# Twelve instead of eight pairs of projection tiles by seven half products in an encoder layer, with some sums and row exchanges by transfers and shifted priorities

## The chip, the core and the metric

The kernel runs on one core of one Trainium2 chip. The core has five engines with queues of their own: TensorE (PE, matmuls; PEld is its weight load), VectorE (DVE), ScalarE (ACT), GpSimd (POOL) and SyncE (SP, which here only issues transfers). Transfers are issued from SP's queue, and from POOL's where they add to what is at the destination (`accum_op`). On-chip memory is SBUF; matmuls write to eight banks of PSUM. The metric is the device time of one execution in microseconds (us), and the median of several executions is compared.

## What is computed

One encoder layer on x of 512 tokens by 1024 features, in float32. The reference, cut to what matters:

```python
proj = h @ w_in[l]
qa, ka, va, qb, kb, vb = jnp.split(proj, SPLITS, axis=-1)   # 1024, 256, 256, 768, 768, 768 wide
# partial rotary on qa, ka, qb, kb (first 16 of 64 dims)
o_a = windowed_gqa_sink(qa, ka, va, a_sink[l])              # 16 heads, 4 kv heads, |i-j| <= 128
o_b = dilated_mixture(qb, kb, vb)                           # 3 groups of 4 heads, merged by denominators
gates = jax.nn.sigmoid(h @ w_gate[l] + b_gate[l])
g_a, g_b = jnp.split(gates, N_BRANCH, axis=-1)
mixed = g_a * (o_a @ w_br_a[l]) + g_b * (o_b @ w_br_b[l])
h = layer_norm(DN_ALPHA * h + mixed @ w_out[l], ln1_g[l], ln1_b[l])
f = (jax.nn.silu(h @ w_ff_gate[l]) * (h @ w_ff_up[l])) @ w_ff_down[l]
h = layer_norm(DN_ALPHA * h + f, ln2_g[l], ln2_b[l])
```

## The kernel before

**Arithmetic.** Each float32 operand is split into a high part (a copy to the type fp32r) and a low part (the difference). A product is three matmuls: high by high, high by low, low by high. The copy for the high part goes to ACT or DVE, the subtraction for the low part always to DVE.

**Dense tiles.** The weights lie in DRAM as units of 128 x 1024. A projection tile (128 output features by all 512 tokens) is `feat_x` (L533): eight slices of the inner dimension times three matmuls of 512 columns (L523 to L525), so 24. Its weights come in two halves of 128 x 512 (256 KB), each loaded on SP's queue and split by `split` (low part at L399). A tile is finished either straight from PSUM (gates by `gate`, L1238; the first query tiles by `rotate`) or copied to SBUF by ACT (`in_sbuf`).

**Pairs.** `pair_x` computes two tiles at once as a two by two block product by Strassen's scheme in Winograd's form: the inner dimension and the tokens are each halved, and seven half products do the work of eight. A half product is four slices times three matmuls of 256 columns (L639 to L641). On the weights' side it needs A11, A12 and A22 as loaded, S1 and S3 (sums of two loaded parts, made by a load on SP and a second, accumulating load issued from POOL, L387), and S2 = S1 + A11 and S4 = A12 + S2 (sums by `form`, with `tt`, on DVE at L544). All seven are then split (`parts`: the high part on ACT at L373, the low part on DVE at L544). On x's side the four sums T1 to T4 are made once by `x_forms` (the step X) and split into `XP`. The order of products is A11, A12, S2, S1, S3, S4, A22. Results are gathered from two banks by four ACT copies of 256 columns (`keep`, L647) and two DVE operations (a `tt` and L662). The feed-forward half uses the same scheme in `quad` (L1690 to L1692).

**Rotary.** `rotate` turns a whole tile on DVE by four operations. For tiles in SBUF, `turn_rows` (the step R) gathers the 16 rows of each head that turn into one tile G by small transfers on SP (L712), makes the exchanged rows H from G by a shuffle on DVE (L715), multiplies both by cosines and sines, adds, and sends the rows back (L723).

**Attention.** `unit_a` (steps A0 to A3, four blocks each) does near attention for one kv head: scores, a masked reduction on DVE (L1022) that needs a sink column copied by POOL (L1020), exponentials on ACT (L1026), normalisation on ACT or DVE (L961, L963), transposes on PE (L973) and products with the values (L1039, L1040). The outputs go to DRAM (`oaD`) and come back in the steps O with an accumulating load (L1308). `unit_b` (B0 to B3) does the dilated mixture for one head slot.

**Gates.** Of 16 gate tiles, two (8 and 9) are computed along with the first tiles, and the rest in the order 10 to 15, 0 to 7. Gates 11 to 15, which come out of pairs, are put away to DRAM (L1229) and fetched back in the branch stage (L1401).

**What sets the order.** The kernel's text records operations with a priority; `Program.run` then plays them against a model of the engines and emits them, so the order on each engine is fixed when the program is built. An operation's priority is `pr.T`, the matmul time recorded so far, plus its own offset (weight loads and splits have -130, `LOOK`). `ORDER` lists the steps: VA, V0 and V12 are values, q, k, Q and K query and key tiles, g gates, P a pair, R turned rows, L a change of the room for weights. Rooms bound how far work runs ahead: `N_WSA` slots for loaded weights, `N_WHLA` for split ones, two slots for each half product. After the attention come the branches, the output projection with the first layer norm, and the feed-forward half with the second. They are the same in both versions.

Of the kernel before, what the change touches and what calls it, by code (L numbers as in the profile page):

```python
# [15 lines left out]
P = 128  # L16
# [35 lines left out]
BIAS = 0.2  # L52
SPARE, SPARE2 = 12, 12
ROOMS = {2: dict(whl=16), 3: dict(whl=20, ws=8)}
# [39 lines left out]
PACK = -60.0  # L94
BY_DMA = ()
AWAY = range(8, 16)
N_WSA, N_WHLA = 8, 16
PAIR_DMA = ()
# [210 lines left out]
def dve(n, fast=False, extra=0.0):  # L309
    return 0.069 + (0.00052 if fast else 0.00104) * n + extra  # L310
# [21 lines left out]
def hybrid_layer(ctx: ExitStack, tc: tile.TileContext, wpack, xT, xtok, sink, bgate,  # L332
# [260 lines left out]

    def pair_x(ua, ub):

# [105 lines left out]

    def turn_rows(tiles):


        c, s_ = packed()
        G, H = slot(), slot()
        n = 32 * len(tiles)
        gs = []
        for i, R in enumerate(tiles):
            for h in range(2):  # L710
                gs.append((G, 2 * i + h))
                op([(SP, 0.1)], lambda e, R=R, i=i, h=h: nc.sync.dma_start(  # L712
                    G.t[32 * i + 16 * h:32 * i + 16 * h + 16], R.t[64 * h:64 * h + 16]), reads=[(R, 1), (R, 2)], writes=[gs[-1]], prio=EV)
        g, h_ = (lambda: G.t[0:n]), (lambda: H.t[0:n])
        op([(DVE, dve(S, extra=0.03))], lambda e: nc.vector.stream_shuffle(h_(), g(), SHUF2), reads=gs, writes=[H], prio=EV)  # L715
        op([(DVE, dve(S))], lambda e: nc.vector.tensor_tensor(g(), g(), c.t[0:n], op=ALU.mult),
           reads=[*gs, *[(c, i) for i in range(4)]], writes=gs, prio=EV)
        op([(DVE, dve(S))], lambda e: nc.vector.tensor_tensor(h_(), h_(), s_.t[0:n], op=ALU.mult),
           reads=[H, *[(s_, i) for i in range(4)]], writes=[H], prio=EV)
# [155 lines left out]

    def turned_values(u, nt, turn_by=0, done=None):

        src = []
        w = S // nt
        for i in range(2):  # L880
            ps = done
            if i or not done:
                ps = bank("dense")
                feat_x(ps, unit(u + i))
            t = slot()

            def evac(e, t=t, ps=ps):
                for a in range(2):
                    s = ps.t.rearrange("p (r t i a) -> p a t r i", a=2, r=2, t=nt)[:, a]
                    d = t.t.rearrange("p (t a r i) -> p a t r i", a=2, r=2, t=nt)[:, a]  # L890
                    if turn_by:
                        copy(e, d[:, turn_by:], s[:, :nt - turn_by])
                        copy(e, d[:, :turn_by], s[:, nt - turn_by:])
                    else:
                        copy(e, d, s)

            op(cp_alts(S, True, 0.3 if turn_by else 0.1)[:2 if turn_by else 1], evac, reads=[ps], writes=[t], prio=VAL if i else NORM)
            src.append(t)
        res = []
        for b in range(NR):  # L900
            pb = bank("tb")

            def turn(e, pb=pb, b=b):
                for i in range(2):
                    nc.tensor.transpose(pb.t[:, i * P:(i + 1) * P], src[i].t[:, b * P:(b + 1) * P], ident.t)

            op([(PE, 0.18)], turn, reads=[*src, ident], writes=[pb])
            res.append(value_split(pb))
        return res
# [57 lines left out]
    def turned_probs(srcs, toks):  # L967

        pb = bank("tb")

        def go(e):
            for i, s in enumerate(srcs):
                nc.tensor.transpose(pb.t[:, i * P:(i + 1) * P], s(), ident.t)  # L973

        op([(PE, 0.36)], go, reads=[*toks, ident], writes=[pb])
        h, l = slot(F32R, "att"), slot(F32R, "att")
        op(cp_alts(S, True), lambda e: copy(e, h.t, pb.t), reads=[pb], writes=[h, (l, "room")])
        op([(DVE, dve(S))], lambda e: nc.vector.tensor_tensor(l.t, pb.t, f32(h.t), op=ALU.subtract),
           reads=[pb, h], writes=[l])
        return h, l  # L980

    def turned_pairs(srcs, toks):
# [6 lines left out]

        op([(PE, 0.36)], go, reads=[*toks, ident], writes=[pb])  # L990
        xs = []
# [59 lines left out]
    def unit_b(hs, q, k, v0, v1, v2):  # L1051
# [98 lines left out]

        dil = []
        for half in range(2):
            xs = turned_pairs([lambda r=r, g=g: pd[r // 2].t[:, (r % 2) * 256 + (g - 1) * P:(r % 2) * 256 + g * P]
# [4 lines left out]
            def pv(e, half=half, xs=xs, od=od):  # L1158
# [6 lines left out]
            op([(PE, 4 * pe(256))], pv, reads=[y for x in xs for y in vtok(x)] + [  # L1165
                y for vs in (v1, v2) for t in vs[2 * half:2 * half + 2] for y in vtok(t)], writes=[od])
            t = slot(F32, "att")
            dil.append(t)
            part = lambda od=od: od.t.rearrange("p (r i a) -> p r a i", r=2, a=2)
            sums = lambda t=t: t.t[0:64, 0:256].rearrange("p (r i) -> p r i", r=2)  # L1170
# [12 lines left out]
        for ms in ((1, 2), (3, 0)):  # L1183
# [17 lines left out]
            op([(PE, 4 * 0.1195)], pv, reads=[hh, ll] + [x for m in ms for x in vtok(v0[m])], writes=[o])  # L1201
        t = slot(F32, "att")
        op(cp_alts(S, True), lambda e: copy(e, t.t[0:64], o.t[64:128]), reads=[o], writes=[t])
        a = 64 * (hs % 2)
        op([(DVE, dve(S))], lambda e: nc.vector.tensor_tensor(t.t[0:64], o.t[0:64], t.t[0:64], op=ALU.add),
# [59 lines left out]
    for f in range(N_ALONG):  # L1265
        gate(8 + f, ps=along[f])
    ka = k_near(psk, 4)
    qa = q_near(psq, 4, (0, 0))
    load(mB, maskb, prio=0)
# [42 lines left out]
    def units_of(w):  # L1312
# [8 lines left out]
        if w[0] == "q":  # L1321
            return U_QA + i, lambda t: qa.extend(q_post(t, 4, ((i // 2) % 2,) * 2))
        if w[0] == "k":
            return U_KA + i, lambda t: ka.extend(k_post(t, 4))
        f = (env["gate"] + 8) % 16
# [3 lines left out]
    def step(w):  # L1329
        if w == "X":  # L1330
            x_forms()
        elif w == "L":
            op([(POOL, 0.0)], lambda e: pr.limits.update(ws=N_WS, whl=N_WHL), after=[env["mark"]])
        elif w[:2] == "P:":
            both = [units_of(x) for x in w[2:].split(",")]
            for (u, f), t in zip(both, pair_x(*[u for u, _ in both])):
                if u < U_GATE:
                    env["turn"].append((t, f))
                else:
                    f(t)  # L1340
        elif w[:2] == "T:":
            u, f = units_of(w[2:])
            env["turn"].append((in_sbuf(u), f))
        elif w == "R":
            tiles = [t for t, _ in env["turn"]]
            turn_rows(tiles)
            done_rows.update(tiles)
# [7 lines left out]
        elif w[0] == "q":  # L1355
            i = int(w[1])
            kv = (i // 2) % 2
            qa.extend(dense_q(U_QA + i, 4, (kv, kv)))
        elif w == "k1":
            ka.extend(dense_k(U_KA + 1, 4))  # L1360
        elif w[0] == "A":
            g = int(w[1])
            for b in range(NR):
                unit_a(g, b, qa[4 * g:4 * g + 4], ka[g], env["va"])
        elif w[0] in "gG":
# [3 lines left out]
        elif w[0] in "QK":  # L1369
            pair, g = int(w[1]), int(w[2])  # L1370
            u, f = units_of(w)
            env["turn"].append((in_sbuf(u), f))
        elif w == "V0":
            env["v0"] = turned_values(U_V0, 8, 1)
# [9 lines left out]

    for w in ORDER.split():
        step(w)

    def free_all(e):
# [166 lines left out]
    def turn_h1(t, j, c0, c1, tok):  # L1555
# [6 lines left out]

        op([(PE, 0.36)], go, reads=[z, ident], writes=[pb], prio=NORM)
        c = slice(t * P, (t + 1) * P)
# [481 lines left out]
```

## Time and profile before

| | us |
|---|---|
| median of 3 runs | 727.84 (727.19 to 729.8) |
| span of the profiled execution, first to last instruction | 725.8 |
| length of the attention part, the branch part and the feed-forward part (about) | 340, 80 and 306 |

The profiled execution's span is 2.0 us less than the median, which is what lies around the instructions. The three parts of the span are: the projections and attentions (0 to about 340 us), the branches and the first layer norm (to about 420 us), and the feed-forward half. In the page's row for an engine stand busy us, the share of the span and the number of instructions. In the rows of groups stand line, engine, operation, output<-inputs, shapes and count, then busy us and mean ns of one, then the idle time before them and what ended it. In the timeline a row is the start, the length and the instruction.

### The profile page before, as it was taken

Reading aid. Unit: us, or ns where it says so; the run is one execution under the profiler, and the core shown is the slowest. Engines: PE = TensorE matmul, PEld = TensorE weight load, DVE = VectorE, ACT = ScalarE, POOL = GpSimd, SP = SyncE. Lnnn points to the kernel's source line nnn. Section 1 sums busy time; section 2 is a strip of 40 time slices with the busy share of each in tenths; the row PEclk is TensorE's granted clock in tenths of the full one; section 3 lists DMA queues with packets and bytes.
Section 4 is the critical chain, followed back from the end, with each engine's and each line's share of the span. In section 5 each row is a group of like instructions: output and inputs, shape, how many; then the busy total and the mean of one; then the engine's idle time right before and its main releaser. Section 6 shows DMA issues by size and latency. Waiting matters only on the chain.

```text
span 725.8 us, 14412 instructions
## 1 busy us (share of the span) xinstructions
PE 717.3 (99%) x4767; PEld 666.2 (92%) x4767; DVE 655.6 (90%) x1408; ACT 471.4 (65%) x1077; POOL 134.0 (18%) x297
## 2 busy tenths in 40 slices
PE   9999999999999999999999999999999999999995
PEld 7889999989988888988888999999999999999985
DVE  6999999889997898898967898899999999899987
ACT  5757798868778665666534666756666566666821
POOL 0021211111100731450020021111112211212000
PEclk9999999999999999999999999999999999999998
DMA  8978788856577689965681499676888888979302
GB/s 256 309 155 202 191 213 246 211 135 172 170 192 185 160 228 253 309 217 185 216 209 44 116 267 228 154 199 155 200 254 212 193 215 225 258 184 200 97 30 87
DMA packets 88010, 140.30 MB, mean 193 GB/s; under 512 B 11136, under 2 KB 24064, under 8 KB 87936
## 3 DMA queue, kind: packets, MB, share of 16 engines
q1 hardware_dynamic: 74336, 114.87, 51.7%
q0 software_dynamic: 13328, 24.39, 20.5%
q8 instruction: 37, 0.61, 0.3%
q14 instruction: 37, 0.30, 0.1%
q10 hardware_dynamic: 272, 0.13, 0.1%
HBM read 114.97 MB, written 7.60 MB: 169 GB/s over the span
## 4 chain that ended last, share of the span: by engine, by line
PE 99%; DVE 1%; DVEq 0%; issue 0%
PE ps L1692 10%; PE ps L1691 9%; PE ps L1690 9%; PE ps L523 9%; PE ps L524 9%; PE ps L525 9%; PE ps L1901 4%; PE ps L1903 4%; PE ps L1902 4%; PE ps L641 3%; PE ps L640 3%; PE ps L639 3%; PE ps L973 3%; PE ps L1480 3%; PE ps L1481 3%; PE ps L1482 3%
## 5 line engine op out<-in xcount | busy, mean ns | idle before, releaser
L373 ACT ACTIVATE sl<-sl 128x512 fp32r<-128x512 f32 (+3 forms) x419 | 230.8, 583 | 59.7 <-DVE sl L544 31.1
L544 DVE TENSOR_TENSOR sl<-sl,sl 128x512 fp32r<-128x512 f32 (+3 forms) x378 | 222.4, 621 | 5.1 <-ACT sl L373 3.4
L373 ACT ACTIVATE sl<-ps 128x256 f32<-128x256 f32 (+5 forms) x209 | 88.7, 445 | 91.6 <-PE ps L1692 56.8
L387 POOL DMA_DIRECT2D sl<-wpack x60 | 53.1, 885 | 342.9 <-DMA sl<-wpack 118.2
L1691 PE MATMUL ps<-sl,sl 128*128 128x256 f32 x352 | 96.8, 275 | 0.0
L1692 PE MATMUL ps<-sl,sl 128*128 128x256 f32 x352 | 96.8, 275 | 0.0
L1690 PE MATMUL ps<-sl,sl 128*128 128x256 f32 x352 | 96.8, 275 | 0.0
L523 PE MATMUL ps<-x,sl 128*128 128x512 f32 (+1 forms) x241 | 93.9, 389 | 0.0
L525 PE MATMUL ps<-x,sl 128*128 128x512 f32 (+1 forms) x241 | 91.4, 379 | 0.0
L524 PE MATMUL ps<-x,sl 128*128 128x512 f32 (+1 forms) x209 | 79.5, 380 | 0.0
L1690 PE MATMUL ps<-x,sl 128*128 128x256 f32 x264 | 72.6, 275 | 0.0
L1691 PE MATMUL ps<-x,sl 128*128 128x256 f32 x264 | 72.6, 275 | 0.0
L1692 PE MATMUL ps<-x,sl 128*128 128x256 f32 x264 | 72.6, 275 | 0.0
L1691 PEld LDWEIGHTS ps<-sl,sl 128*128 128x128 f32 x352 | 67.6, 192 | 0.1
L1690 PEld LDWEIGHTS ps<-sl,sl 128*128 128x128 f32 x352 | 67.6, 192 | 0.1
L1692 PEld LDWEIGHTS ps<-sl,sl 128*128 128x128 f32 x352 | 67.6, 192 | 0.0
L399 DVE TENSOR_TENSOR sl<-sl,sl 128x512 fp32r<-128x512 f32 x94 | 62.8, 682 | 1.8 <-ACT sl L373 1.3
L525 PEld LDWEIGHTS ps<-x,sl 128*128 128x128 f32 x241 | 45.9, 190 | 6.5
L1690 PEld LDWEIGHTS ps<-x,sl 128*128 128x128 f32 x264 | 50.6, 192 | 0.4
L1691 PEld LDWEIGHTS ps<-x,sl 128*128 128x128 f32 x264 | 50.6, 192 | 0.4
L523 PEld LDWEIGHTS ps<-x,sl 128*128 128x128 f32 x241 | 46.0, 191 | 5.4 <-ACT sl L373 0.3
L1692 PEld LDWEIGHTS ps<-x,sl 128*128 128x128 f32 x264 | 50.7, 192 | 0.0
(172 smaller groups left out, 1851.0 us busy)
## 6 DMA issues: line engine op xcount, KB each, us to landing
sl<-wpack SPq DMA_DIRECT2D x249, 256.0 KB, 3.9
sl<-wpack POOLq DMA_DIRECT2D x60, 256.0 KB, 5.3
sl<-sl SPq DMA_DIRECT2D x110, 128.0 KB, 3.1
wf<-wpack SPq DMA_DIRECT2D x51, 256.0 KB, 5.2
wf<-wpack POOLq DMA_DIRECT2D x24, 256.0 KB, 6.2
oa<-sl SPq DMA_DIRECT2D x32, 128.0 KB, 3.6
sl<-sl SPq DMA_DIRECT2D x68, 32.0 KB, 2.6
sl<-oa SPq DMA_DIRECT2D x8, 256.0 KB, 5.1
```

The lines of the kernel that those rows point to most:

```text
L373: nc.scalar.activation(dst, src, AF.Copy)
L387: op([(POOL, 1.0)], lambda e: nc.gpsimd.dma_start(b.t, src2, accum_op=ALU.add), reads=[b], writes=[b], prio=prio, moves=1.65)
L399: op([(DVE, dve(S))], lambda e: nc.vector.tensor_tensor(l.t, src.t, f32(h.t), op=ALU.subtract), reads=[src, h], writes=[l], prio=prio, abs ...
L523: mm(o, a, x0, start=(k == 0 and begins), stop=False, skip_group_check=split)
L524: mm(o, a, x1, start=False, stop=False, skip_group_check=split)
L525: mm(o, b, x0, start=False, stop=(k == nk - 1), skip_group_check=split)
L544: op([(DVE, dve(w))], lambda e: nc.vector.tensor_tensor(dst(), x(), y(), op=o), reads=reads, writes=writes, prio=prio)
L1690: mm(o, wh, pairs(bh[k]()), start=(first and k == 0), stop=False, skip_group_check=True)
L1691: mm(o, wh, pairs(bl[k]()), start=False, stop=False, skip_group_check=True)
L1692: mm(o, wl, pairs(bh[k]()), start=False, stop=(k == 3), skip_group_check=True)
L1901: mm(ps.t, x0, pairs(w[0].t), start=(first and m == 0), stop=False, skip_group_check=True)
L1902: mm(ps.t, x0, pairs(w[1].t), start=False, stop=False, skip_group_check=True)
```

## The change

The number of steps P or D in `ORDER` goes from 8 to 12. A pair can now mix a query or key tile with a gate. Pairs marked D make the sums S2 and S4 by accumulating transfers from SBUF to SBUF, issued from POOL, instead of by DVE. Steps marked r make H by further small transfers on SP instead of the shuffle. A step may carry `@n`, which shifts the priority of all that it records by n (us of matmul time, negative is earlier). Gates 8 to 10 are now put away as well. Three constants change, and two costs that the planner assumes for transposes. `SUM_BY_DMA` stays empty and the step PV isn't used, so that what hangs on them (in `unit_b` and `turned_values`) emits nothing; `qa` and `ka` become dictionaries.

```diff
-SPARE, SPARE2 = 12, 12
+SPARE, SPARE2 = (10, 12)
 ORDER = """
-VA q1 A0 q2 q3 g X P:k1,q4 R A1 P:q5,g P:q6,q7 R A2 P:g,g A3 P:g,g L P:Q00,K00 R V12 P:Q01,K01 R P:Q02,K02 R V0 B0 Q10 K10 R Q11 K11 R B1 O O Q12 K12 R O O B2 B3 O O O O g8
+q1@-778 VA@-8 X@-496 A0@-58 q2@-14 P:q3,g@6 R@-96 D:k1,q4@8 R@72 P:q5,Q01@-338 D:q6,q7@-15 D:g,g@21 r@471 P:g,Q00 L@-4 A1@-8 P:g,K00@-17
+A3@19 A2@-16 R@321 V12@15 P:g,K01@13 R@9 P:Q02,K02@4 R@13 V0@50 B0@1 P:K10,Q12@9 R@-52 K11@5 P:Q10,Q11 R@6 B1@-20 O@-83 O@1 O@-56 O@-622
+K12@6 g@-17 O@-20 r@-507 O@34 O@30 g@16 g@34 g@22 B2 O P:g,g@-15 B3@1 g@-43 g@5
 """
-FORMS = -60.0
+FORMS = -120.0
-N_WSA, N_WHLA = 8, 16
+N_WSA, N_WHLA = (8, 18)
...
-    def pair_x(ua, ub):
+    def pair_x(ua, ub, by_dma=False):
...
         def form(key, of, x, y):
+            if by_dma:
+                a, b = W[of], W[x if y == of else y]
+                op([(POOL, 1.0)], lambda e: nc.gpsimd.dma_start(a.t, b.t, accum_op=ALU.add), reads=[a, b], writes=[a],
+                   prio=-LOOK, moves=1.65)
+                W[key] = a
+                return
             tt(lambda: W[of].t, lambda: W[x].t, lambda: W[y].t, ALU.add, [W[x], W[y]], [W[of]], S, -LOOK)
...
-    def turn_rows(tiles):
+    def turn_rows(tiles, by_dma=False):
...
+        hs_ = [H]
+        if by_dma:
+            hs_ = []
+            for i, R in enumerate(tiles):
+                for h in range(2):
+                    for z in range(2):
+                        hs_.append((H, 4 * i + 2 * h + z))
+                        op([(SP, 0.1)], lambda e, R=R, i=i, h=h, z=z: nc.sync.dma_start(
+                            H.t[32 * i + 16 * h + 8 * z:32 * i + 16 * h + 8 * z + 8], R.t[64 * h + 8 - 8 * z:64 * h + 16 - 8 * z]),
+                           reads=[(R, 1), (R, 2)], writes=[hs_[-1]], prio=EV)
+        else:
+            op([(DVE, dve(S, extra=0.03))], lambda e: nc.vector.stream_shuffle(h_(), g(), SHUF2), reads=gs, writes=[H], prio=EV)
...
-        op([(PE, 0.36)], go, reads=[*toks, ident], writes=[pb])
+        op([(PE, 0.436)], go, reads=[*toks, ident], writes=[pb])
...
     def gate(f, ps=None):
...
+        if f in AWAY:
+            put_away(f)
...
-        elif w[:2] == "P:":
+        elif w[:2] in ("P:", "D:"):
...
-            for (u, f), t in zip(both, pair_x(*[u for u, _ in both])):
+            for (u, f), t in zip(both, pair_x(*[u for u, _ in both], w[0] == "D")):
...
-        elif w == "R":
+        elif w in "Rr":
             tiles = [t for t, _ in env["turn"]]
-            turn_rows(tiles)
+            turn_rows(tiles, w == "r")
...
     for w in ORDER.split():
+        w, _, later = w.partition("@")
+        pr.T += float(later or 0)
         step(w)
+        pr.T -= float(later or 0)
```

More of the change, by code (lines that the diff above doesn't have):

```diff
@@ L95 @@
 BY_DMA = ()
+SUM_BY_DMA = ()
 AWAY = range(8, 16)
-N_WSA, N_WHLA = 8, 16
+N_WSA, N_WHLA = (8, 18)
 PAIR_DMA = ()
@@ L873, in scores, with turned_values @@
         return go, [(qt, "h"), (qt, "l"), (kt, "h"), (kt, "d"), (kl, "h"), (kl, "d")]
-    def turned_values(u, nt, turn_by=0, done=None):
+    def turned_values(u, nt, turn_by=0, done=None, made=None):
         src = []
@@ L880, in turned_values, with order @@
         for i in range(2):
+            if made:
+                t, z = slot(), made[i]
+                def order(e, t=t, z=z):
+                    s = z.t.rearrange("p (r t i) -> p t r i", r=4, t=nt)
+                    d = t.t.rearrange("p (t r i) -> p t r i", r=4, t=nt)
+                    copy(e, d[:, turn_by:], s[:, :nt - turn_by])
+                    copy(e, d[:, :turn_by], s[:, nt - turn_by:])
+                op([(ACT, act(S) + 0.1)], order, reads=[(z, 1), (z, 2)], writes=[t], prio=VAL if i else NORM)
+                src.append(t)
+                continue
             ps = done
@@ L1151, in unit_b @@
         dil = []
+        add_up = hs in SUM_BY_DMA
+        E = [slot(F32, "att"), slot(F32, "att")] if add_up else []
         for half in range(2):
```

44 lines of the change are left out of this document (30 added, 14 removed).

## The prediction, made before the run

> **What bounds the kernel now.** I read the table of cores first, then the page's busy line and its chain, then what TensorE (PE) waited for.
>
> ```profile
> core 0: 725.8 us, clock 0.996
> PE 717.3 (99%) x4767; PEld 666.2 (92%) x4767; DVE 655.6 (90%) x1408; ACT 471.4 (65%) x1077; POOL 134.0 (18%) x297
> PE 99%; DVE 1%; DVEq 0%; issue 0%
> PE ps L459 <- DVE eps L510: 1.2, 1, 1.2
> ```
>
> The chain that ended last is PE almost from end to end, at full granted clock, and the list of PE's waits has one entry, 1.2 us at the very start. So time can only come out of the number of matmuls and their spacing, and anything else matters only once it makes PE wait. A busy PE is not proof of that, since matmul ends are modelled; the proof is the spacing of their starts. From the timeline of PE, first and last of 62 rows of dense projections, and then of 127 rows of half products:
>
> ```profile
> 19.69 0.38 PE L525 MATMUL ps<-x,sl 128*128 128x512 f32 x1
> ...
> 32.85 0.38 PE L523 MATMUL ps<-x,sl 128*128 128x512 f32 x1
> 423.83 0.28 PE L1691 MATMUL ps<-sl,sl 128*128 128x256 f32 x1
> ...
> 437.90 0.28 PE L1691 MATMUL ps<-sl,sl 128*128 128x256 f32 x1
> ```
>
> A 512-wide matmul costs 13.16/61 = 0.2157 us, a 256-wide one 14.07/126 = 0.1117 us; the second stretch also shows that half products run with no hole for 14 us on end.
>
> The second engine near its limit is VectorE (DVE). By stage (columns: window, length, busy us of PE, PEld, DVE, ACT, POOL, then clock, DMA share, GB/s):
>
> ```profile
> 0.00:80.00 80.00, 78.81 (x440) 69.63 (x441) 72.09 (x157) 54.61 (x120) 12.45 (x25) 1.00 0.80 222
> 80.00:200.00 120.00, 120.00 (x899) 114.54 (x898) 110.54 (x259) 96.35 (x237) 18.80 (x52) 1.00 0.73 195
> 200.00:340.00 140.00, 140.00 (x775) 125.39 (x774) 121.79 (x336) 96.64 (x248) 43.84 (x152) 1.00 0.77 217
> 420.00:680.00 260.00, 260.00 (x2037) 251.56 (x2037) 245.66 (x472) 167.82 (x361) 49.42 (x57) 1.00 0.82 207
> ```
>
> DVE is at 90%, 92% and 87% in the three stretches that the change rearranges, and at 245.66/260 = 94.5% in the feed-forward stretch, where PE waits for nothing. 94.5% is therefore a load that this kernel is seen to carry.
>
> **The change part by part.** *Four more pairs.* Two dense projection tiles are 48 matmuls of 512 columns, 48 x 0.2157 = 10.36 us. A pair is seven products of 12 matmuls of 256 columns, 84 x 0.1117 = 9.38 us. One pair saves 0.98 us and four save 3.90 us, all on the path. The number of transposes, scores and attention products is unchanged, and the feed-forward half is not touched. The constants 0.36 to 0.436 and 0.18 to 0.218 only tell the planner what a transpose costs; they add no instruction.
>
> *What the pairs ask of DVE and ACT.* The rows, within 0 to 340 us:
>
> ```profile
> L399 DVE TENSOR_TENSOR sl<-sl,sl 128x512 fp32r<-128x512 f32 x70 | 47.0, 682 | 1.8 <-ACT sl L373 1.3 <-DMA sl<-sl 0.4
> L544 DVE TENSOR_TENSOR sl<-sl,sl 128x512 f32<-128x512 f32 x16 | 10.9, 683 | 0.0
> L544 DVE TENSOR_TENSOR sl<-sl,ps 128x512 f32<-128x512 f32 x8 | 5.5, 685 | 0.1
> L662 DVE SCALAR_TENSOR_TENSOR sl<-ps,sl 128x256 f32<-128x256 f32 x8 | 3.3, 418 | 0.7 <-ACT sl L1026 0.6
> L715 DVE STREAM_SHUFFLE sl<-sl 64x512 f32<-64x512 f32 x7 | 5.1, 732 | 0.0
> L373 ACT ACTIVATE sl<-sl 128x512 fp32r<-128x512 f32 x151 | 90.4, 622 | 16.8 <-DVE sl L747 7.2 <-DVE sl L570 2.7 <-DVE sl L1211 1.7
> L647 ACT ACTIVATE sl<-ps 128x256 f32<-128x256 f32 x32 | 12.0, 375 | 3.7 <-PE ps L641 3.6
> ```
>
> Two dense tiles need four low parts, 4 x 0.68 = 2.73 us of DVE. A pair needs seven, the two weight sums S2 and S4 (the 16 rows of L544, two for each of the eight pairs) and two merges of results: 9 x 0.68 + 0.69 + 0.42 = 7.25 us. So a pair adds 4.5 us of DVE, four add 18.1. Three pairs marked D hand both sums to transfers: 6 x 0.683 = 4.1 us less. Two exchange steps marked r lose their shuffle: 1.5 us less. Net +12.5 us of DVE. On ACT a pair adds three copies and four evictions, 3 x 0.62 + 4 x 0.375 = 3.4 us, 13.5 for four, less four evictions of dense tiles that go (0.6 each), about 11 us on an engine with 92 us to spare before 340 us.
>
> Where this falls decides whether it is hidden. Up to the first dilated unit there are nine pairs where eight were, three of them with transferred sums: 4.5 - 4.1 - 0.7, no change. After that come three new pairs in the stretch 200 to 340: 121.8 + 3 x 4.52 - 0.73 = 134.6 us of DVE in 140 - 2.9 = 137 us, or 98%. That is over 94.5%, unless work moves to ACT. What can move there are the copies and scalings that the planner may give to either engine:
>
> ```profile
> 200.00:340.00 140.00, 8.61 (x22) 1.00 0.77 217
> 200.00:340.00 140.00, 5.89 (x19) 1.00 0.77 217
> ```
>
> These are DVE's copies (L375) and normalisations (L963) in that stretch, 14.5 us together; to fall back to 94.5% only 5.1 us of it must move, and ACT has 137 - 96.6 - 8 = 32 us free there. I cost the added DVE and ACT work at nothing; without that cover it is 134.6/0.945 - 137 = 5.4 us.
>
> *Sums by transfer and POOL's queue.* Issues, with the median time to landing, and POOL's own instruction (min/median/max ns):
>
> ```profile
> sl<-wpack POOLq DMA_DIRECT2D x60, 256.0 KB, 5.3
> sl<-oa POOLq DMA_DIRECT2D x8, 256.0 KB, 7.5
> sl<-sl SPq DMA_DIRECT2D x68, 32.0 KB, 2.6
> L387 POOL DMA_DIRECT2D sl<-wpack x60: 848/862/1563, 34.8 to 653.5; - x60
> L1020 POOL COPY sl<-nsink x64: 178/184/1847, 40.1 to 217.0; 128x1 f32<-128x1 f32 x64
> ```
>
> Four pairs bring 8 accumulating loads and the D pairs 6 accumulations within SBUF: 14 x 0.86 = 12 us of POOL, which is 18% busy. An accumulation from SBUF to SBUF is not in the trace; its cost to the path lies between nothing and the delay of a chain. In a D pair S2 waits for S1, and S4 for S2. Each sum takes 0.86 + 5.3 = 6.2 us (by the slower row 8.4) where DVE took 0.68, so S4 is ready 11.0 to 15.4 us later. Behind a waiting accumulation in POOL's order stand the next pair's S1 and S3 and the sink copies of L1020, which DVE's score reductions and so PE's transposes wait for. What hides it is the lead of the weights: 18 slots for split halves (N_WHLA, 16 before) are nine products of 12 x 0.1117 = 1.34 us, 12.1 us. I take the nearer row, 11.0, which that lead just covers: cost nothing.
>
> The Trainium skill, "DMA: Bandwidth & Descriptors", section "Anatomy of one DMA", gives such a POOL-issued transfer 2.0 us plus bytes over 436 GB/s, an estimate of 2.6 us for 256 KB. By that the chain would be 2 x (0.86 + 2.6 - 0.68) = 5.6 us later and well covered. The 5.3 us row is twice that, and I go by the row.
>
> A rule speaks against the change. The Trainium skill, "SBUF — State Buffer", section "SBUF: two separate sides", says that a DVE copy in a two-port mode locks GpSimd out, so that a POOL-issued transfer's descriptors wait. The issue row agrees that an issue can stretch, from 862 to 1563 ns. If all 14 stretched so far, POOL would lose 9.8 us, and PE nothing while the lead holds.
>
> *Row exchanges, gates, order.* The r steps replace a shuffle by 16 and 4 small transfers on SP's queue; each lands in some 2.6 us, beside the ones that the step already waits for, so at best 0.73 us shorter and at worst 20 issues long for the weight loads behind them. Gates 8, 9 and 10 now go to DRAM and come back: 6 x 256 KB. All traffic added (12 weight parts, 6 sums, 6 gate moves, 256 KB each, and the rows) is 6.6 MB, where 340 us at 200 GB/s move 68; the DMA share of 0.73 to 0.80 has room for 10%. Bounds for the two together: nothing, to about 2 us if one load comes late; I take nothing. The shifted priorities reorder work that PE has plenty of; the forms of x, which must now be done for the first pair earlier, had their first sums at 7.6 us already:
>
> ```profile
> L544 DVE TENSOR_TENSOR sl<-sl x4: 415/417/424, 7.6 to 14.7; 128x256 f32<-128x256 f32 x4
> ```
>
> **Sum.** 3.90 us off a span of 725.8 us is 721.9. The median of the runs, 727.84, is 2.0 us above the span, so the floor is 723.9. I add 0.4 us for small new waits, an estimate between none and the single 1.2 us that the trace has: **724.3 us**.
>
> **The rivals.** *DVE becomes the bound between the dilated units* (for: 98% before anything moves; also DVE is nearly full before 80 us, where the pair of q3 adds 4.5. Against: 14.5 us can move, 94.5% is carried). At the full 5.4 us: 723.9 + 5.4 = 729.3; half of it gives 726.6.
>
> *The chain of transferred sums outlasts the lead* (slower). Place: the three D pairs, before the near attention is done. Each falls short by 15.4 - 12.1 = 3.3 us if such an accumulation lands like the oa row. Three times that is 9.9 us: 733.8 us. It decides from a landing of 5.9 us on (2 x (0.86 + 5.9 - 0.68) = 12.1). For: 7.5 is seen. Against: other ready work stands in PE's order between the products, and 5.3 is the median of 60.
>
> *The pairs do not save what they should*: if half products in this stage were spaced 0.1175 us apart half of the gain would go, 725.9. Against it is the 0.1117 us row, from the same kind of product.
>
> **How the numbers follow.** Saved and covered 0.60 (723.5 to 725.3), DVE bound 0.25, sums late 0.12, spacing 0.03. A measurement of this kernel can tell about 0.5% from no change, 3.6 us, so "faster" begins at 724.2: within the likeliest case. Waits under 0.3 us in all would put it there. I split that case 0.38 faster, 0.22 within; DVE and spacing lie within (0.28), of which 0.02 counts as faster for a repeat of the runs' own scatter; late sums are slower. Faster 0.40, within 0.48, slower 0.12. The range starts 0.9 us under the floor (the runs lie 0.65 under to 2.0 over their median) at 723.0 and takes in the DVE case up to 729.3; late sums stay out.
>
> **What would show it.** Right: the matmuls of L639 to L641 rise from 672 to 1008 and the dense ones fall by 192, PE's list of waits stays near one entry, DVE over 92% in 200 to 340 with fewer copies of L375 and L963. DVE bound: PE waits on DVE lines after 200 us. Late sums: PE waits before 200 us on splits that follow a sl<-sl transfer of POOL. The prediction falls if the first matmuls, the tail after the last one, or the feed-forward stretch change in length, for none of these was given a term.

## The result: slower, and the profile after

| | before | after |
|---|---|---|
| median of 5 runs, us | 727.84 (727.19 to 729.80) | 740.15 (737.72 to 743.21) |
| span of the profiled execution, us | 725.8 | 737.7 |

The ratio is 1.0167, with a 95% interval of 1.0145 to 1.0189: slower by 1.7%, outside the predicted range. From the table of cores, the page and its chain of waits, in the order in which they were shown of before:

```profile
core 0: 737.7 us, clock 0.996
PE 718.9 (97%) x4911; PEld 668.8 (91%) x4911; DVE 665.3 (90%) x1418; ACT 482.4 (65%) x1109; POOL 145.4 (20%) x311
PE 77%; DMA 4%; DVE 4%; POOL 3%; ACT 2%; issue 2%; SPq 0%; DVEq 0%; ACTq 0%; POOLq 0%
```

No engine is busier than forecast. DVE gained 9.7 us over the whole span (12.5 were forecast), ACT 11.0 (11), POOL 11.4 (12). But the chain, 99% PE before, now goes through transfers, DVE, POOL and ACT for some 15% of the span. (It can be followed back only to 59.1 us, so 8% are not covered.) The list of what PE waited for had one entry; now its first five are:

```profile
PE ps L1196 <- DVE sl L1030: 2.6, 3, 1.2
PE ps L890 <- DVE sl L791: 2.5, 2, 2.3
PE ps L1239 <- DVE sl L1010: 1.7, 1, 1.7
PE ps L462 <- DVE eps L513: 1.2, 1, 1.2
PE ps L528 <- DVE sl L402: 1.1, 1, 1.1
```

The fourth is the old one at the start. The pairs themselves did what they should. From the groups by line, the dense matmuls of before and then of after, and one group of the half products (L639 before, L648 after), in each kernel:

```profile
L523 PE MATMUL ps<-x,sl 128*128 128x512 f32 (+1 forms) x241 | 93.9, 389 | 0.0
L639 PE MATMUL ps<-sl,sl 128*128 128x256 f32 x128 | 35.5, 277 | 0.0
```

```profile
L526 PE MATMUL ps<-x,sl 128*128 128x512 f32 (+1 forms) x177 | 68.4, 386 | 0.1
L648 PE MATMUL ps<-sl,sl 128*128 128x256 f32 x192 | 53.4, 278 | 0.0
```

64 dense matmuls fewer on each of three lines, 192 in all, and half as many half products again. So the 3.9 us were saved, and about 16 us of new holes (stretches in which PE stands or runs slowly) lie over them. Adding up, over all rows of PE's timeline, what each distance between two starts exceeds the distance in an undisturbed run of its width (0.216, 0.1625 and 0.1117 us for 512, 384 and 256 columns, 0.109 for a transpose) gives 8.2 us before and 24.1 us after. The difference of 15.9, less 3.9, is 12.0; the spans differ by 11.9. By place the excess of after is 4.9 us from 40 to 80 us, 1.8 from 140 to 160, 6.3 from 260 to 300, 4.8 from 300 to 340, 0.9 from 400 to 420, and at most 0.7 in any other 20 us once the start is over. From the table by stage (columns as before):

```profile
40.00:60.00 20.00, 17.52 (x111) 15.75 (x110) 16.90 (x30) 11.19 (x20) 4.60 (x8) 1.00 0.92 227
140.00:160.00 20.00, 19.18 (x107) 16.49 (x106) 17.57 (x44) 13.07 (x34) 3.57 (x12) 1.00 0.87 221
260.00:280.00 20.00, 16.40 (x102) 14.03 (x101) 18.23 (x38) 10.67 (x27) 5.70 (x12) 1.00 0.82 200
320.00:340.00 20.00, 18.11 (x101) 15.65 (x101) 16.63 (x46) 14.22 (x34) 7.53 (x34) 1.00 0.59 195
```

PE waits on DVE in nearly all of these, but DVE has idle time in each of the windows. So the question is what DVE waited for. Its list of waits, from 38 to 60 us, 250 to 280 and 280 to 345:

```profile
DVE sl L547 <- DMA sl<-wpack: 2.8, 1, 2.8
...
DVE sl L735 <- DMA sl<-sl: 3.3, 1, 3.3
...
DVE sl L402 <- ACT sl L376: 4.3, 2, 3.8
DVE st L1158 <- POOL st L1151: 3.0, 2, 2.6
```

These holes have the same shape: one instruction of DVE stands on a late transfer, or on a late copy by POOL or ACT. DVE's order is fixed when the program is built, so what PE needs stands behind the waiting instruction. The first case can be followed row by row. The sum of a pair waited 2.8 us at 44.9 us for its accumulating load. DVE then hardly paused up to 62 us and did not win the time back, and PE stood at 56 us. From the timelines of DVE and then of PE:

```profile
47.67 0.69 DVE L547 TENSOR_TENSOR sl<-sl,sl 128x512 f32<-128x512 f32 x1 [2.82 <-DMA sl<-wpack]
57.71 1.40 DVE L791 TENSOR_TENSOR sl<-sl,sl 64x512 fp32r<-64x512 f32 x2
...
55.86 0.38 PE L528 MATMUL ps<-x,sl 128*128 128x512 f32 x1
58.55 0.35 PE L890 MATMUL ps<-sl,sl 128*128 128x256 f32 x1 [2.31 <-DVE sl L791]
```

This first hole is not a fixed part of the change. The load was issued at 39.2 us and landed at 47.6. Six of the kernels below keep this order, and their edits act only after 50 us. In their profiles the same load was issued at 37.0 to 38.0 us and landed at 43.8 to 45.0, DVE waited for it 0.1 us at most, and the excess from 40 to 80 us is at most 2.0 us instead of 4.9. So of seven profiles with this order only the one shown here has this hole, and why the load was late in it stays open.

In the case at 260 us the shuffle of a step R (L735) waits for gathers of rows (L721), which SP issued one behind the other up to 257.4 us. SP's timeline from 220 to 262 us, of after and then of before: the first and the last row of 62 issues in each, and between them a run of twelve moves of the dilated unit and, of after, the last two gathers of that step:

```profile
219.87 0.59 SPq L743 DMA_DIRECT2D sl<-sl  x1
...
243.74 9.28 SPq L831 DMA_DIRECT2D sl<-sl  x12
...
256.79 1.15 SPq L721 DMA_DIRECT2D sl<-sl  x2
...
261.60 0.68 SPq L731 DMA_DIRECT2D sl<-sl  x1
```

```profile
220.05 0.59 SPq L811 DMA_DIRECT2D sl<-sl  x1
...
242.79 8.44 SPq L811 DMA_DIRECT2D sl<-sl  x12
...
261.56 0.57 SPq L1307 DMA_DIRECT2D sl<-oa  x1
```

DVE's waits of before, from 250 to 280 us, have the same entry:

```profile
DVE sl L715 <- DMA sl<-sl: 1.6, 2, 1.3
```

The twelve issues take 9.28 us after and 8.44 before, 0.77 and 0.70 us each, and the rows of the 62, with the short pauses within them, add up to 39.9 and 39.4 of some 42 us, so the queue has next to no room there in both kernels. The change hardly adds to it at this place; from 100 to 200 us SP's issues take 75.0 us (124 of them) where they took 65.3 (114). DVE waited for late rows in before as well, 1.3 us at most, and PE never noticed. After, it is 3.3 us, and PE does. A queue with next to no room, and a lead that was just enough for one order, is what the profile of before had to tell and what the prediction did not read from it.

### The profile page after: what moved, and what is told of

It reads as the page before. It is cut to its first block, busy times and chain, and to the rows that moved or that the text cites. A ratio compares the mean times of both kernels' runs of the same rounds, so it can differ in the third digit from the quotient of the medians.

```text
span 737.7 us, 14857 instructions
## 1 busy us (share of the span) xinstructions
PE 718.9 (97%) x4911; PEld 668.8 (91%) x4911; DVE 665.3 (90%) x1418; ACT 482.4 (65%) x1109; POOL 145.4 (20%) x311
## 4 chain that ended last, share of the span: by engine, by line
PE 77%; DMA 4%; DVE 4%; POOL 3%; ACT 2%; issue 2%; SPq 0%; DVEq 0%; ACTq 0%; POOLq 0%
PE ps L1747 9%; PE ps L1746 9%; PE ps L1748 9%; PE ps L650 4%; PE ps L649 4%; PE ps L648 4%; PE ps L1957 4%; PE ps L1959 4%; PE ps L1958 4%; PE ps L1537 3%; PE ps L1538 3%; PE ps L1536 3%; PE ps L1005 3%; PE ps L528 2%; PE ps L526 2%; PE ps L527 2%
## 5 line engine op out<-in xcount | busy, mean ns | idle before, releaser
L376 ACT ACTIVATE sl<-sl 128x512 fp32r<-128x512 f32 (+3 forms) x430 | 238.5, 585 | 71.7 <-DVE sl L547 35.7
L547 DVE TENSOR_TENSOR sl<-sl,sl 128x512 fp32r<-128x512 f32 (+3 forms) x408 | 241.4, 627 | 6.9 <-ACT sl L376 3.2
L376 ACT ACTIVATE sl<-ps 128x256 f32<-128x256 f32 (+6 forms) x208 | 86.3, 436 | 79.1 <-PE ps L1748 53.0
L390 POOL DMA_DIRECT2D sl<-wpack x68 | 60.0, 895 | 348.4 <-DVE sl L547 120.9
L1747 PE MATMUL ps<-sl,sl 128*128 128x256 f32 x352 | 96.8, 275 | 0.0
L1748 PE MATMUL ps<-sl,sl 128*128 128x256 f32 x352 | 96.8, 275 | 0.0
L1746 PE MATMUL ps<-sl,sl 128*128 128x256 f32 x352 | 96.8, 275 | 0.0
L528 PE MATMUL ps<-x,sl 128*128 128x512 f32 (+1 forms) x177 | 67.4, 381 | 1.1 <-DVE sl L402 1.1
L526 PE MATMUL ps<-x,sl 128*128 128x512 f32 (+1 forms) x177 | 68.4, 386 | 0.1
L402 DVE TENSOR_TENSOR sl<-sl,sl 128x512 fp32r<-128x512 f32 x78 | 52.4, 684 | 4.9 <-ACT sl L376 4.6
L527 PE MATMUL ps<-x,sl 128*128 128x512 f32 (+1 forms) x145 | 55.0, 380 | 0.1
L547 DVE TENSOR_TENSOR sl<-sl,ps 128x512 f32<-128x512 f32 (+1 forms) x71 | 46.6, 660 | 8.4 <-PE ps L1959 5.3
L648 PE MATMUL ps<-sl,sl 128*128 128x256 f32 x192 | 53.4, 278 | 0.0
L650 PE MATMUL ps<-sl,sl 128*128 128x256 f32 x192 | 52.8, 275 | 0.0
L649 PE MATMUL ps<-sl,sl 128*128 128x256 f32 x192 | 52.8, 275 | 0.0
L1747 PEld LDWEIGHTS ps<-x,sl 128*128 128x128 f32 x264 | 50.6, 192 | 0.4
```

The costliest lines, as they stand in the source:

```text
L376: nc.scalar.activation(dst, src, AF.Copy)
L390: op([(POOL, 1.0)], lambda e: nc.gpsimd.dma_start(b.t, src2, accum_op=ALU.add), reads=[b], writes=[b], prio=prio, moves=1.65)
L526: mm(o, a, x0, start=(k == 0 and begins), stop=False, skip_group_check=split)
L527: mm(o, a, x1, start=False, stop=False, skip_group_check=split)
L528: mm(o, b, x0, start=False, stop=(k == nk - 1), skip_group_check=split)
L547: op([(DVE, dve(w))], lambda e: nc.vector.tensor_tensor(dst(), x(), y(), op=o), reads=reads, writes=writes, prio=prio)
```

## The experiments

Two theories stood at the start. **SP**: time to issue in SP's queue is what ran out, and late transfers reach PE through DVE's order. **Sums/DVE**: the transferred sums of the D pairs, or DVE's load, are late, which were the prediction's rivals. A third, **slack**, said that the planner's new price of a transpose reorders the work badly by itself.

### The two loads on SP, and the two rivals

In the kernels of this part and the next two that are made from the changed one, the order of the other instructions was kept. `e1_rows_shuffled` makes H in the two r steps by a DVE shuffle again:

```diff
-                        op([(SP, 0.1)], lambda e, R=R, i=i, h=h, z=z: nc.sync.dma_start(
-                            H.t[32 * i + 16 * h + 8 * z:32 * i + 16 * h + 8 * z + 8], R.t[64 * h + 8 - 8 * z:64 * h + 16 - 8 * z]),
+                        op([(SP, 0.1)], lambda e: None,
...
+            if by_dma:
+                nc.vector.stream_shuffle(h_(), g(), SHUF2)
             nc.vector.tensor_tensor(g(), g(), c.t[0:n], op=ALU.mult)
```

> The changed kernel with its order kept on every engine; only the 20 small transfers of the two r steps are gone from SP's queue, and DVE makes the exchanged rows by two shuffles (0.73 us each) instead. Theory SP (SP's queue issues without pause at about 0.70 us each and what it brings comes late for DVE and ACT, behind which PE waits): 20 x 0.70 = 14 us less of SP's queue, so 2 to 4 us less than the change, 736 to 738. Rival DVE (DVE is the bound): 1.5 us more DVE, 740 to 742. Rival sums (the accumulations within SBUF come late): no difference, 740.

Measured: 735.73 us (733.95 to 737.04), ratio to before 1.0103 [1.0082, 1.0124]. 20 small transfers fewer, two shuffles more for the busy DVE: 4.4 us less than the change by the medians.

`e1_stores_by_pool` issues the 32 stores of near attention's outputs from POOL:

```diff
-            op([(SP, 0.73)], lambda e, part=part: nc.sync.dma_start(
+            op([(SP, 0.73)], lambda e, part=part: nc.gpsimd.dma_start(
```

> The changed kernel with its order kept; the 32 stores of near attention's outputs are issued from POOL's queue instead of SP's, the same bytes to the same places. Theory SP: 32 x 0.70 = 22 us less of SP's queue, 4 to 6 us less than the change, 734 to 736, and the wait of DVE for gathered rows at 257 us shorter. Rival POOL (POOL's queue holds up the sink copies and the accumulating loads): 32 x 0.86 us more of it, 742 to 746. Rival DVE and rival sums: 740.

Measured: 735.06 us (731.53 to 738.44), 1.0102 [1.0053, 1.0150], 5.1 us less than the change, with the same bytes; the interval just touches the change's. Where DVE meets the shuffle that waited at 260 us, in the changed kernel, in this one and in the one with shuffled rows:

```profile
260.15 0.01 DVE L735 LOAD_MASK_SELECT sl<-sl  x1 [3.32 <-DMA sl<-sl]
254.02 0.01 DVE L735 LOAD_MASK_SELECT sl<-sl  x1 [0.54 <-DMA sl<-sl]
260.34 0.01 DVE L734 LOAD_MASK_SELECT sl<-sl  x1 [1.81 <-DMA sl<-sl]
```

With the stores moved, the rows come 6.1 us earlier; some 3 of these are holes before 240 us that this profile does not have. With shuffled rows they do not come earlier, and the wait is shorter only because DVE gets there later: 16 of the 20 transfers taken away lie before 108 us and the other four behind this shuffle, at 261.6 us, and the excess from 260 to 300 us is 6.7 us where the changed kernel has 6.3. That profile has 3.1 us less excess from 40 to 80 us and 3.5 less from 300 to 340, and 2.5 more from 160 to 200. The 4.4 us are measured, then, but they are not traced to this queue at any one place.

`e1_sums_on_dve` takes the D pairs' transfers away and makes the six sums by DVE:

```diff
-                op([(POOL, 1.0)], lambda e: nc.gpsimd.dma_start(a.t, b.t, accum_op=ALU.add), reads=[a, b], writes=[a],
+                op([(POOL, 1.0)], lambda e: nc.vector.tensor_tensor(a.t, a.t, b.t, op=ALU.add), reads=[a, b], writes=[a],
```

> The changed kernel with its order kept; the six sums S2 and S4 of the three D pairs are made by DVE at the place where POOL issued them. Theory SP: 739 to 741, since SP's queue is as before. Rival sums: the waits before 200 us go, 3 to 5 us less, 735 to 737. Rival DVE: 4.1 us more DVE, 741 to 744.

Measured: 739.62 us (737.63 to 741.56), 1.0165 [1.0139, 1.0191], no different from the change. The trace of the change agrees: its six sums are issued from 60.7 to 118.0 us and land in 3.3 to 7.3 us, and PE has no wait on its list from 60 to 140 us. Neither the chain of transferred sums nor 4.1 us of DVE is what costs the time. `e1_before_transposes` is the kernel before with the planner's prices of a transpose alone, of which one is shown:

```diff
...
-        op([(PE, 0.36)], go, reads=[*toks, ident], writes=[pb])
+        op([(PE, 0.436)], go, reads=[*toks, ident], writes=[pb])
...
```

> The kernel before with one part of the change alone: the planner counts a transposing group at 0.436 us instead of 0.36. The work is the same, the order differs a little. Theory slack (the kernel before is free of waits because its plan counts PE's time too short, so that on the chip everything else has up to 4 us more time than planned): 729 to 731, with waits of PE after 100 us. If the plan's slack doesn't matter: 727.5 to 728.5, with no waits.

Measured: 728.11 us (727.30 to 729.46), 1.0004 [0.9994, 1.0013]. The price does nothing to that kernel. In the changed order it was not taken back alone.

### Both reliefs, and the cost put into the kernel before

`e2_both` joins the first two edits.

> The changed kernel in its own order, with both reliefs of SP's queue at once: the 20 exchange transfers of the r steps are shuffles of DVE again, and the 32 stores of near attention's outputs are issued from POOL. Alone each gave back about 4.5 us of 12.3. Theory SP (the queue of SP is too full for this order, and DVE's queue stands on what lands late): the two add up, since they lie in different places: 730 to 733. Rival 'one stall' (each relief cures the same stall): no better than the better one alone, 735. What stays over 724 by theory SP are the stalls that do not come from SP: DVE's wait for the accumulating load at 45 us, and POOL's late sink copies and cross sums.

Measured: 733.02 us (731.01 to 735.50), 1.0068 [1.0047, 1.0088]. 7.1 us come back of 12.3. That is less than the 9.5 of the two alone, but the interval of the moved stores is 3.5 us wide to either side, so whether the two overlap is not shown. And 4.2 us of the excess that this profile has less than the changed kernel's lie from 40 to 80 us, where the edits do not reach; 3.0 lie from 260 to 300. What still made PE wait, and DVE's longest wait of another kind, from 255 to 345 us:

```profile
PE ps L1242 <- DVE sl L1013: 1.9, 1, 1.9
PE ps L1199 <- DVE sl L1033: 1.8, 2, 1.6
...
DVE st L1161 <- POOL st L1154: 3.3, 2, 2.8
```

The converse is the sharper test: 34 transfers which nothing waits for go into the kernel before, in SP's queue (`e2_more_by_sp`) or in POOL's (`e2_more_by_pool`).

```diff
+                    nc.sync.dma_start(dram.tile([16, S], F32, name=name("again")), c.t[0:16])
```

> The kernel before in its own order, with 34 further transfers of 32 KB (16 rows of the cosines to a place in DRAM that nothing reads), one behind each gather of rows, issued on SP. Nothing waits for them; they only stand in SP's queue. Theory SP: each takes about 0.7 us of a queue that is close to full between 140 and 340 us, 34 x 0.7 = 24 us of issuing in some eight clumps of two or four; what lands later then makes DVE and so PE wait: +5 to +17 us, 733 to 745. Rival 'order' (the loss comes from the order of the changed kernel, not from SP's load): within 0.5% of before, 727 to 730. Rival 'bytes': 1.1 MB more of 140 MB, nothing that can be measured.

> The same 34 transfers in the kernel before, issued from POOL instead of SP. Same bytes, same places, other queue. Theory SP: 34 x 0.86 = 29 us more on a queue that is 18% busy; a sink copy or an accumulating load can stand behind up to four of them (3.4 us): 727 to 731, at least 4 us under the same transfers on SP. Rival 'bytes': the same time as on SP.

Measured: on SP 735.53 us (734.49 to 735.91), 1.0097 [1.0082, 1.0112]; on POOL 728.85 us (727.16 to 730.27), 1.0005 [0.9994, 1.0016]. Same bytes, same places, and only the queue decides: 7.6 us against nothing that can be measured. DVE's waits from 255 to 280 us, on SP and then on POOL:

```profile
DVE sl L718 <- DMA sl<-sl: 3.5, 1, 3.5
```

```profile
DVE sl L718 <- DMA sl<-sl: 1.9, 2, 1.6
```

The gather that this shuffle waits for is issued at 257.30 us on SP and at 254.42 on POOL, and the shuffle starts at 260.00 and 257.28; up to 240 us the two profiles have the same excess, 8.9 us. So here the way from the queue to DVE can be followed. On SP the shuffle waits as long as in the changed kernel, and the excess from 260 to 280 us is 5.9 us, where the changed kernel has 5.1 and the kernel before 0.4; another 2.3 lie from 100 to 120 us. On average an issue that carries nothing of the computation costs 7.6/34 = 0.22 us of the kernel's time there.

### POOL's share, and ACT's

Two edits of `e2_both` go after the waits that are not SP's. `e3_cross_by_act` gives half of the dilated units' small copies to ACT, `e3_sinks_by_act` the sink copies:

```diff
-                    nc.gpsimd.tensor_copy(st.t[y, 8 + b:25 + b:16], st.t[x, 4 + r:21 + r:16])
+                    nc.scalar.copy(st.t[y, 8 + b:25 + b:16], st.t[x, 4 + r:21 + r:16])
```

```diff
-            op([(POOL, 0.13)], lambda e, p=p, c=c: nc.gpsimd.tensor_copy(p.t[:, n:n + 1], nsink.t[:, c:c + 1]),
+            op([(POOL, 0.13)], lambda e: None,
...
+                nc.scalar.copy(p.t[:, n:n + 1], nsink.t[:, c:c + 1])
                 nc.scalar.activation(p.t[:, :n + 1], p.t[:, :n + 1], AF.Exp, bias=st.t[:, h:h + 1], scale=-1.0,
```

> The kernel of e2_both (the changed kernel's order, both reliefs of SP, 733.0), with half of the small copies of the dilated units (32x2, 64 of 128) made by ACT instead of POOL. In e2_both VectorE stood 2.8 us near 320 us on the last of these copies, and PE behind it 1.9 us. In the trace of the changed kernel such a copy takes 0.18 us, but 0.56 us while VectorE runs an addition or subtraction with both operands in SBUF. Theory POOL late: the wait near 320 goes, 1.5 to 3 us faster than e2_both: 730 to 731.5. Rival 'next in line' (another late operand stands right behind it): 732.5 to 733.5. ACT has the time there, so slower than 733.5 is not expected by either.

> The kernel of e2_both, with the 64 sink copies (128x1) of near attention made by ACT, each directly ahead of its exponential, instead of by POOL. In e2_both ACT stood 1.9 us near 150 us on a sink copy of POOL, VectorE 1.7 us on ACT, and PE lost 1.8 us. Theory POOL late: that stall goes, but 64 x some 0.2 us = 13 us of work come to ACT between 40 and 220 us, where it is 84% busy: 731 to 733. Rival 'ACT in place of POOL': the stall stays or moves, 733 to 736.

Measured: cross copies by ACT 737.38 us (736.46 to 739.88), 1.0131 [1.0115, 1.0148]; sinks by ACT 732.65 us (730.08 to 740.55), 1.0074 [1.0050, 1.0098]. The first is a miss for both theories: 4.4 us slower than `e2_both`. ACT's new work, and then DVE's waits from 250 to 345 us:

```profile
L1154 ACT COPY st<-st 32x2 f32<-32x2 f32 x64 | 12.2, 191 | 0.8
```

```profile
DVE sl L402 <- ACT sl L376: 4.3, 5, 1.3
```

12.2 us on an engine that is busy 65% of the time made the copies behind them late, and DVE's low parts wait for those (five times here, in `e2_both` once from 250 to 345 us). The second edit took its own hole away (1.8 us of excess from 140 to 160 us before it, under 0.6 after) without a gain that can be measured.

### Twelve pairs in other orders

If the pairs are sound and the order is what fails, another order must bring most of the time back. `e2_other_order` has the changed kernel's code with SP's issue priced at 0.72 us in the planner, and steps and offsets chosen for that:

```diff
-SPARE, SPARE2 = (10, 12)
+SPARE, SPARE2 = (8, 12)
-q1@-778 VA@-8 X@-496 A0@-58 q2@-14 P:q3,g@6 R@-96 D:k1,q4@8 R@72 P:q5,Q01@-338 D:q6,q7@-15 D:g,g@21 r@471 ...
+q1@-718 VA@-8 q2@-14 A0@-9 X@-455 P:q3,g r@-263 D:k1,q4@8 R@155 D:g,g@31 P:q5,Q01@-264 P:q6,q7@-15 R@461 ...
-FORMS = -120.0
+FORMS = -80.0
-N_WSA, N_WHLA = (8, 18)
+N_WSA, N_WHLA = (8, 16)
-                        end = now + (0.62 if 14 < now < SLOW else 0.47)
+                        end = now + (0.72 if 14 < now < SLOW else 0.47)
```

> Twelve pairs with the code of the changed kernel, but another order of steps, offsets and rooms (SPARE 8, N_WHLA 16, FORMS -80), chosen with SP's issue priced at 0.72 us in the planner instead of 0.62. One step r instead of two; the near units A2 and A3, and the steps O, lie further apart. Theory SP/order: the pairs' 3.9 us are real and what took 16 us was the order's lack of slack towards SP: 723.5 to 726.5. Rival 'pairs' (twelve pairs ask more of SP, DVE and POOL than any order can hide): 732 or more.

Measured: 729.45 us (727.98 to 733.87), 1.0024 [1.0010, 1.0038]. That is 10.7 us less than the change, with all twelve pairs, but 3 us more than theory SP wanted and no gain over before. Its profiled execution, the fastest of the twelve, has a span of 726.0 us, as before, with 12.0 us of excess against 8.2: the pairs' 3.9 us are there, and 3.8 us of waits eat them. From 380 to 420 us the excess is 2.6 us, where before has 0.7, so that half of the 3.8 lie there, where PE waits for the first layer norm:

```profile
PE ps L1615 <- DVE sl L1597: 1.4, 2, 0.8
```

`e3_order_spare` is a third order, chosen to bear slower engines:

```diff
+q1@-632 X@-474 VA@-8 q2@-14 A0 P:q3,g r@-513 D:k1,q4@8 D:g,g@31 R@190 P:q5,Q01@-434 P:q6,q7@-15 R@471 ...
```

> Twelve pairs with the changed kernel's code in a third order (as e2_other_order: SPARE 8, N_WHLA 16, SP's issue priced at 0.72; FORMS -100), chosen so that it also bears VectorE and ScalarE 1 to 3% slower than planned and SP up to 0.12 us slower per issue. Theory SP/order: the tighter the order, the more of the pairs' 3.9 us is lost; this one should lose about 1 to 2 us less than e2_other_order (729.45) and come out at 726.5 to 728.5, that is not over the kernel before. Rival 'floor' (what e2_other_order still loses has nothing to do with slack): 729 to 730 again.

Measured: 731.26 us (729.62 to 733.14), 1.0042 [1.0027, 1.0056], not the gain that was expected. It lost 5.8 us from 280 to 300 us, the longest piece on rows that came back late, where PE itself waits for the transfer:

```profile
PE ps L888 <- DMA sl<-sl: 2.2, 1, 2.2
```

Last, the relief that gave the changed kernel 5 us, put on the best order (`e4_order_and_pool`, the same edit as in `e1_stores_by_pool`):

> The best order so far (e2_other_order, 729.45; its code and order kept) with the 32 stores of near attention's outputs issued from POOL instead of SP, the relief that gave the changed kernel 4.5 us. Theory SP: if what this order still loses of the pairs' 3.9 us is lost to SP's queue, 726 to 728, faster than the kernel before by up to 0.25%. Rival 'elsewhere': its trace shows 2.5 of the lost microseconds in the branch stage near 395 and 404 us, where PE waits for VectorE's layer norm and SP has little to do, and the rest in pieces under 1 us: 729 to 730, no gain.

Measured: 740.31 us (738.85 to 741.65), 1.0167 [1.0149, 1.0185]: 11 us worse, which no theory expected. One hole makes nearly all of it. PE's longest wait, DVE's longest from 260 to 300 us, and POOL's sums over the six stretches of 5 us from 240 to 270 us:

```profile
PE ps L646 <- DVE sl L669: 9.7, 1, 9.7
```

```profile
DVE sl L400 <- DMA oa<-sl: 10.2, 2, 8.9
```

```profile
sum 30.00, POOL 26.98; mean POOL 4.50
```

In this order the last near unit falls together with the dilated units' copies, and POOL is busy for 27 of those 30 us. The stores that were moved stand behind these copies, and DVE stands 8.9 us until one of them has landed. So a queue is relieved into another only where that one has room at that place; POOL's 20% over the whole span of the changed kernel said nothing of it. No version tried here beats the kernel before.

## Why the prediction was wrong, point by point

*What bounds the kernel, and what the pairs save*: right. PE's list and its spacing were the right views, and 3.90 us were saved: in the fastest execution of the best order the span equals that of before with 3.8 us more of holes. The terms that the prediction left out held: the first matmul starts at 1.2 us in both, 7.7 and 7.6 us lie behind the last one's start, and no new hole lies after 420 us.

*DVE's and ACT's load*: right in size and in its answer. The whole-span sums grew by 9.7 and 11.0 us, and six sums more on DVE cost nothing (`e1_sums_on_dve`). Its sign was not met: over 92% of DVE from 200 to 340 us was to be seen, and the stretch reads

```profile
200.00:340.00 140.00, 133.54 (x841) 120.70 (x840) 120.66 (x319) 101.13 (x264) 45.81 (x156) 1.00 0.82 226
```

120.66/140 = 86%, since DVE stood there and some of its work slid past 340 us. The prediction argued from DVE's busy share; DVE became the engine that PE waits for (that rival's sign, after 200 us too) while it was itself idle, on late operands.

*Sums by transfer*: costed at nothing, and nothing it was, by the same experiment. The slower rival named this mechanism and 733.8 us; only its direction came true, by another mechanism. The hole at 56 us, before 200 us as its sign asked, followed a load from DRAM that came late, and the first sum was issued only at 60.7 us.

***Row exchanges, gates, order***: this is the step that failed. It said "at worst 20 issues long for the weight loads behind them", "the DMA share of 0.73 to 0.80 has room for 10%", bounds of "nothing, to about 2 us if one load comes late; I take nothing". The share of the DMA engines tells how busy these are; what was short was SP's time to issue, which the step never summed, though the trace of before shows 62 issues in 39.4 us from 220 to 262 us. The clearest size is that of the converse test, 7.6 us for 34 idle issues in the kernel before. In the changed kernel taking the row exchanges off SP gave 4.4 us, moving 32 stores out of its queue 5.1, and both 7.1, of which the profiles place only a part at SP's late rows. The last sentence, that the shifted priorities "reorder work that PE has plenty of", failed with it: PE had plenty of work, but it came through DVE's order, and another order of the same work gives 10.7 us back.

*The sum*: the 0.4 us for "small new waits" stood for what became 15.9 us. A single entry in PE's list of waits was read as slack; it only says that each lead was long enough, not by how much. The hole at 56 us, which six other profiles of this order lack, is no part of this step.

What stays open: of the 9 us by which `e2_both` still lies above the floor of 723.9, no single cause was isolated. The rows show POOL's copies, ACT's copies and late loads in pieces of 1 to 3 us, and the two edits that went after them moved the wait or made it longer. The 6.8 MB that the changed kernel moves more are a rival that no run takes away in this order: from 40 to 60 us its DMA share is 0.92 where before has 0.65. Alone they do not make the loss, since `e2_other_order` moves 146.3 MB, 0.8 less than the changed kernel, and loses 3.8 us to new holes instead of 15.9.

## What to carry to other kernels

Before transfers are added to an in-order queue, sum its issues against time, stage by stage, as for an engine: bytes and DMA share do not show a queue that has no room to issue. Where the bottleneck engine never waits, look one step back at how long its feeders already wait for their operands; that they waited 1.3 us here without a hole in PE says that the lead covers so much, and not that it covers more. A relief is bought in the queue that takes the work over, so read that queue at the same place, not over the whole span.

## What the runs showed of the hardware

A hole in PE can cost more than its length. After the 2.5 us that it lost between the starts at 55.86 and 58.55 us, the granted clock fell to a half, and 256-wide products were spaced 0.211 us for some 3.4 us. By stretches of 2 us, of the changed kernel:

```profile
58.00:60.00 2.00, 1.29 (x7) 1.07 (x8) 1.94 (x4) 1.48 (x3) 0.00 (x0) 0.98 0.79 261
60.00:62.00 2.00, 2.00 (x10) 1.91 (x9) 2.00 (x7) 1.09 (x4) 1.26 (x2) 0.50 0.11 35
62.00:64.00 2.00, 2.00 (x14) 2.00 (x13) 0.91 (x3) 1.23 (x5) 0.47 (x1) 0.67 0.90 141
64.00:66.00 2.00, 2.00 (x20) 2.00 (x19) 2.00 (x5) 1.16 (x3) 0.90 (x1) 1.00 0.81 120
```

Ten matmuls in 2 us instead of twenty: by an estimate, half of 3.4 us at half the clock, another 1.7 us lost. The Trainium skill, "TensorE: Matmul & The Clock Gate", section "HAM oscillation — how this bites in real kernels", sums this up as no idle gaps of PE over about 3.4 us. Here a hole of 2.5 us, with a second of 0.3 us behind it, was enough in one case; the measurement decides, so holes shorter than the rule's are not safe in this kernel.

Small copies of POOL are stretched by some operations of DVE. In the timelines of POOL and DVE of the changed kernel, about 323 us:

```profile
322.12 0.18 POOL L1151 COPY st<-st 32x2 f32<-32x2 f32 x1
322.33 0.65 POOL L1150 COPY st<-st 32x2 f32<-32x2 f32 x1
322.93 0.66 POOL L1151 COPY st<-st 32x2 f32<-32x2 f32 x1
323.63 0.56 POOL L1150 COPY st<-st 32x2 f32<-32x2 f32 x1
324.23 0.19 POOL L1151 COPY st<-st 32x2 f32<-32x2 f32 x1
...
321.66 0.68 DVE L1469 SCALAR_TENSOR_TENSOR sl<-sl,ps 128x512 f32<-128x512 f32 x1
322.26 1.89 DVE L402 TENSOR_TENSOR sl<-sl,sl 128x512 fp32r<-128x512 f32 x3
324.06 0.58 DVE L995 TENSOR_SCALAR sl<-sl,st 128x192 f32<-128x192 f32 x2
```

A copy takes 0.18 us beside an operation with an operand in PSUM, and 0.56 to 0.66, the length of the subtraction, beside one with both operands in SBUF. The Trainium skill, "SBUF — State Buffer", section "SBUF: two separate sides", states that a DVE operation with two SBUF inputs and a GpSimd operation that reads SBUF exclude each other for a whole instruction; the rows agree. This kernel's commonest DVE operation is of that kind, so POOL's copies, which DVE waits for, are stretched where DVE does most of it.
